# Two-layer decoder trunk on one core: a bank of its own for the second half's scale in the heads, own tiles for output-projection and head weights, background steps elsewhere, tables stored by GpSimd

## The chip, the core and the metric

The kernel runs on one core of one Trainium2 chip. The metric is device time in microseconds (us) of one launch. The core's engines are called by the names that the profile uses: PE (TensorE, matrix products), DVE (VectorE), ACT (ScalarE), POOL (GpSimd) and SP (SyncE, which here only starts transfers). Each engine works through its own list of instructions in order; the lists meet in semaphores.

## The reference

Input `x` is one sequence of 512 positions with 1024 channels, `c` one conditioning vector. Everything is float32.

```python
mod = silu(c) @ w_mod[i] + b_mod[i]              # shift, scale and gate, six vectors of 1024 per layer
h = rms_norm(x, norm_mix[i]) * (1 + sc1) + sh1
layer 0: y = stick_breaking_attention(h, w_qkv, w_o)     # 16 heads of 64, causal
layer 1: u = h @ w_in ; y = diagonal complex state space (64 groups of 16 channels, 64 states) + d_skip * u
         z = gelu(y) ; y = (z * sigmoid(z @ w_glu + b_glu)) @ w_o
x = x + g1 * y
h = rms_norm(x, norm_ffn[i]) * (1 + sc2) + sh2
up = causal_conv3(h @ w_up) + conv_b             # 2 x 2816 columns
x = x + g2 * ((silu(gate half) * value half) @ w_down)
out = rms_norm(x, norm_out) * (1 + sc) + sh      # after both layers
```

## The kernel before, in words

Activations lie transposed: `x[k]`, k = 0 to 7, is a tile of 128 channels by 512 positions, and a product's weights are the stationary operand. To keep float32 accuracy every operand is split into a high and a low part, and `mm3` (L160, L163, L164) makes one product out of three matmuls: high by high, high weights by the low part of the activations (`hL`, `gL`), low weights (`*_l`) by the high part. So a weight block of 512 KB takes four steps before PE can use all of it: SP loads it (`*_r`, L152), ACT copies it to the high part (`*_h`, L154), DVE subtracts to the low part (`*_l`, L155). Split weights live in rings of NW = 5 blocks, loaded ones in a ring of 3.

The modulation vectors are matrix-vector products that nobody needs at once. They run in the background: a step `bg` is one load of 512 KB (`wg`, L184) on SP's queue and one DVE instruction (L185) that multiplies and sums it. Where a `bg` call stands in the program decides where that DVE instruction lies in DVE's list.

The stages in order are: norm and q/k/v products with attention windows (to about 250 us); the attention's output projection `w_o`, by `out_proj`; layer 0's conv-FFN, in three groups of 8, 8 and 6 units (a unit is two up blocks, the convolution on ACT and DVE, and the pair `gH`, `gL`; after a group come its down products); the state-space (SSM) layer; layer 1's conv-FFN; the last norm.

**Heads.** The product that follows a norm cannot start before the whole residual stream is known, so it starts in halves of 256 positions. `out_proj` finishes the first half of all tiles, `rstd_stat` sums the squares (`acc`) with a column matmul on PE, takes the root on ACT and finishes on DVE, `rstd_bc` (L275) spreads the result over all partitions with a matmul into a bank `rbc`, and `norm_tile` makes one tile of the normed input: a DVE product with `rbc` (`nt`, L293), two ACT instructions (`hH` L300, and L302), a DVE subtraction (`hL`, L306). `head_mm` makes these tiles in turn and feeds them to the first four up blocks (ffn0, ffn1) or the first blocks of `w_in`. The first HEADK tiles run in halves, the others at full width. Before the change both halves of the scale share one bank.

**Order.** A scheduler with a simulated timeline arranges the instructions of each engine. The program binds it in places: `pe_pin` keeps program order on PE, `follow` keeps it on another engine or queue, `behind_head` and `issue_after` put work behind a named instruction. Constants HEADB, HEADW, UPRE and USTG say behind which product of a head something is put: the second half's scale, the weight splits of the next blocks, the first SSM stages.

**Tables.** During ffn0, POOL computes the SSM tables in two passes into a scratch tile `tb`; each pass stores two blocks of 512 KB to device memory (`sR`, L969), through SP's queue. After the second pass `ball` (L983), which goes into the scratch's space, is loaded and POOL builds `bl` from it, which SP stores to `sB` (L1002).

## Time and profile before

| | us |
|---|---|
| median of 3 runs (lowest, highest) | 1208.41 (1207.86, 1210.76) |
| profiled execution, its own time | 1208.56 |
| its span, first to last instruction | 1206.5 |
| PE busy | 1169.9 (97%) |
| DVE busy | 884.0 (73%) |
| ACT busy | 564.4 (47%) |
| POOL busy | 264.8 (22%) |
| mean granted clock of PE | 0.992 |

Times of the sums in the prediction are those of the profiled execution: 1206.5 us of span and 2.1 us around it. In a row of the timeline stand the start in us, the duration, the engine, the line, the operation, the tiles written and read, the operands' shape and how many instructions the row folds together; brackets give the idle time of that engine just before, and what ended it. In a row of the windows view stand a stretch of time, its length, and for PE, PEld, DVE, ACT and POOL the busy time and the instructions, then the granted clock, the share of the DMA engines and GB/s.

### The profile page before, as it was taken

Reading aid. Unit: us, or ns where it says so; the run is one execution under the profiler, and the core shown is the slowest. Engines: PE = TensorE matmul, PEld = TensorE weight load, DVE = VectorE, ACT = ScalarE, POOL = GpSimd, SP = SyncE. Lnnn points to the kernel's source line nnn. Section 1 sums busy time; section 2 is a strip of 40 time slices with the busy share of each in tenths; the row PEclk is TensorE's granted clock in tenths of the full one; section 3 lists DMA queues with packets and bytes.
Section 4 is the critical chain, followed back from the end, with each engine's and each line's share of the span. In section 5 each row is a group of like instructions: output and inputs, shape, how many; then the busy total and the mean of one; then the engine's idle time right before and its main releaser. Section 6 shows DMA issues by size and latency. Waiting matters only on the chain.

```text
span 1206.5 us, 16354 instructions
## 1 busy us (share of the span) xinstructions
PE 1169.9 (97%) x6182; PEld 960.6 (80%) x6182; DVE 884.0 (73%) x1298; ACT 564.4 (47%) x884; POOL 264.8 (22%) x241
## 2 busy tenths in 40 slices
PE   8999999979999999989999999999999999999997
PEld 6886777668788877868888878789888888888887
DVE  6968988485896489996877579876598457744655
ACT  6756667346553123422445657644554234422443
POOL 1000000000098799999720000000000000000003
PEclk9999999999999999999999999999999999999999
DMA  8875653261244767878754599652157438432222
GB/s 312 311 247 172 194 176 121 62 234 37 70 124 131 251 237 218 249 232 277 251 174 159 171 303 340 212 169 63 66 178 243 123 110 202 157 117 76 79 79 70
DMA packets 93536, 210.99 MB, mean 175 GB/s; under 512 B 19601, under 2 KB 39953, under 8 KB 93458
## 3 DMA queue, kind: packets, MB, share of 16 engines
q1 hardware_dynamic: 85138, 207.86, 54.0%
q10 hardware_dynamic: 8320, 2.10, 0.8%
q8 instruction: 48, 0.79, 0.3%
q14 instruction: 30, 0.25, 0.1%
HBM read 188.68 MB, written 21.24 MB: 174 GB/s over the span
## 4 chain that ended last, share of the span: by engine, by line
PE 66%; DVE 12%; DMA 7%; POOL 6%; issue 3%; ACT 3%; SPq 1%; POOLq 0%; ACTq 0%; DVEq 0%
PE up L163 10%; PE up L164 10%; PE up L160 10%; PE dn L160 5%; PE dn L163 5%; PE dn L164 5%; DMA wg<-in_w_modT_dram 3%; DVE wg L185 2%; DVE up_l L155 2%; PE wos L160 1%; DVE ca L445 1%; PE wos L164 1%; PE wos L163 1%; DVE om L728 1%; PE o L758 1%
## 5 line engine op out<-in xcount | busy, mean ns | idle before, releaser
L164 PE MATMUL up<-hH,up_l 128*128 128x512 f32 (+1 forms) x692 | 264.4, 384 | 4.3 <-DVE up_l L155 4.2
L163 PE MATMUL up<-hL,up_h 128*128 128x512 f32 (+1 forms) x692 | 264.3, 384 | 0.4 <-DVE hL L306 0.2
L160 PE MATMUL up<-hH,up_h 128*128 128x512 f32 (+1 forms) x692 | 260.7, 384 | 1.2 <-ACT hH L300 1.1
L445 DVE SCALAR_TENSOR_TENSOR ca<-up,small,ca 128x511 f32<-128x511 f32 (+1 forms) x176 | 131.4, 747 | 81.8 <-ACT ca L443 78.9
L185 DVE SCALAR_TENSOR_TENSOR wg<-wg,cact 128x1024 f32<-128x1024 f32 x96 | 123.8, 1305 | 43.9 <-DMA wg<-in_w_modT_dram 43.7
L164 PEld LDWEIGHTS up<-hH,up_l 128*128 128x128 f32 x692 | 130.0, 188 | 32.0 <-DVE up_l L155 6.4
L163 PEld LDWEIGHTS up<-hL,up_h 128*128 128x128 f32 x692 | 130.0, 188 | 26.0 <-DVE hL L306 0.9
L160 PEld LDWEIGHTS up<-hH,up_h 128*128 128x128 f32 x692 | 127.9, 188 | 28.1 <-ACT hH L300 1.5
L163 PE MATMUL dn<-gL,dn_h 128*128 128x512 f32 (+1 forms) x394 | 145.0, 368 | 2.7 <-DVE gL L460 2.7
L160 PE MATMUL dn<-gH,dn_h 128*128 128x512 f32 (+1 forms) x394 | 145.2, 370 | 0.5 <-ACT gH L459 0.5
L164 PE MATMUL dn<-gH,dn_l 128*128 128x512 f32 (+1 forms) x394 | 144.8, 368 | 0.0
L154 ACT ACTIVATE up_h<-up_r 128x1024 fp32r<-128x1024 f32 x84 | 88.3, 1053 | 118.1 <-PE dn L163 39.3
L155 DVE TENSOR_TENSOR up_l<-up_r,up_h 128x1024 fp32r<-128x1024 f32 x84 | 127.9, 1523 | 21.3 <-ACT up_h L154 15.2
L1342 POOL TENSOR_SCALAR xa<-x,Anorm_out 128x256 f32<-128x256 f32 x7 | 5.7, 819 | 577.7 <-ACT dn_h L154 562.8
L443 ACT ACTIVATE ca<-up,small 128x512 f32<-128x512 f32 x88 | 67.9, 771 | 95.0 <-PE up L164 95.0
L163 PEld LDWEIGHTS dn<-gL,dn_h 128*128 128x128 f32 x394 | 74.4, 189 | 15.1 <-DVE gL L460 3.0
L160 PEld LDWEIGHTS dn<-gH,dn_h 128*128 128x128 f32 x394 | 74.5, 189 | 13.6 <-ACT gH L459 0.9
L164 PEld LDWEIGHTS dn<-gH,dn_l 128*128 128x128 f32 x394 | 74.6, 189 | 12.2
L336 DVE SCALAR_TENSOR_TENSOR x<-dn,mod,x 128x512 f32<-128x512 f32 (+1 forms) x55 | 37.3, 678 | 60.8 <-PE dn L164 60.8
L452 ACT ACTIVATE ca<-ca 128x512 f32<-128x512 f32 x44 | 27.9, 633 | 89.7 <-DVE ca L445 88.0
L154 ACT ACTIVATE dn_h<-dn_r 128x1024 fp32r<-128x1024 f32 (+1 forms) x48 | 46.6, 982 | 49.1 <-PE dn L163 35.4
L155 DVE TENSOR_TENSOR dn_l<-dn_r,dn_h 128x1024 fp32r<-128x1024 f32 (+1 forms) x48 | 63.9, 1331 | 2.7 <-ACT dn_h L154 2.5
(306 smaller groups left out, 2256.1 us busy)
## 6 DMA issues: line engine op xcount, KB each, us to landing
wg<-in_w_modT_dram SPq DMA_DIRECT2D x96, 512.0 KB
up_r<-in_w_up_dram SPq DMA_DIRECT2D x84, 512.0 KB
dn_r<-in_w_down_dram SPq DMA_DIRECT2D x32, 512.0 KB
wgs<-in_w_modT_dram SPq DMA_DIRECT2D x16, 512.0 KB
dn_r<-in_w_down_dram SPq DMA_DIRECT2D x16, 384.0 KB
wv_r<-in_w_v_dram SPq DMA_DIRECT2D x8, 512.0 KB
wk_r<-in_w_qk_dram SPq DMA_DIRECT2D x8, 512.0 KB
wq_r<-in_w_qk_dram SPq DMA_DIRECT2D x8, 512.0 KB
```

What stands on the lines that cost most here:

```text
L154: order("S", lambda: S.activation(wh[:, :n], raw[:, :n], AF.Copy))
L155: pin["split"] = order("V", lambda: V.tensor_tensor(wl[:, :n], raw[:, :n], wh[:, :n].bitcast(F32), ALU.subtract))
L160: ins = PE.matmul(ps, ah, bh, start=start, stop=False)
L163: PE.matmul(ps, ah, bl, start=False, stop=False)
L164: PE.matmul(ps, al, bh, start=False, stop=stop)
L185: mul = lambda: V.scalar_tensor_tensor(w, w, 1.0, cact, ALU.mult, ALU.mult, accum_out=raw[:, col:col + 1])
L336: add = lambda: V.scalar_tensor_tensor(xs, pv, gate, xs, ALU.mult, ALU.add)
L443: follow("S", lambda: S.activation(ca, ps, AF.Identity, bias=small[:, cb:cb + 1], scale=tapw[2]))
L445: follow("V", lambda: V.scalar_tensor_tensor(ca[:, q:], ps[:, :T - q], tapw[2 - q], ca[:, q:], ALU.mult, ALU.add))
L452: follow("S", lambda: S.activation(cg, cg, AF.Silu))
L728: pin["scan"] = V.tensor_tensor_scan(om[:, :n][:, ::-1], om[:, :n][:, ::-1], maskb[:, T - n:][:, ::-1], 1.0, ALU.mult, ALU.max)
L758: ins = PE.matmul(po[pr][h2 * HD:(h2 + 1) * HD, j * P:], vn[:, j, hd:hd + HD], src, start=j == 0, stop=j == 3)
```

## The change

It has five parts.

1. **Heads.** The second half's scale gets a bank of its own, from the pool of product banks. HEADK goes from 5 to 6 tiles in halves. The normed tiles of the first half are made two ahead of the products that use them. The second half's statistics stand behind the second product of tile 1, before they stood ahead of tile 2. The last two tiles, at full width, are scaled in two halves because the scale lies in two banks. HEADW, UPRE (10 to 12) and USTG (7, 8 to 6, 7) follow.
2. **Weights around w_o.** The last attention window prefetches three blocks of `w_o` and not four, and has 4 background steps and not 6. `out_proj` for `w_o` has tiles of its own for blocks 5 and 6 (over space that attention has left) and loads the first four up blocks itself, as `upo0` to `upo3`, as the other two heads did already. The five background steps inside it are gone.
3. **Background steps.** The seven steps removed there, and one from the second group and one from the third, go elsewhere. ffn0 has 6, 0 and 3 of them in its groups; it had 0, 3 and 4. Others go into the SSM layer's last stages and the tiles behind them.
4. **Tables.** `sR` is stored through GpSimd's own queue, no longer through SP's.
5. **SSM.** `run(2)` in place of `run(1)` puts two units of the GLU product between a scan and the transposes behind it. The loads of the maps (`pB`, `pR`, `pT`, `pC`) are tied into one order.

On DVE, in the `w_o` projection, from the projection's first residual sums to the statistics (`x_78` to `x_85` are the tiles of the residual stream, `wg` the background steps, `acc` the sum of squares), before:

```order
L336 SCALAR_TENSOR_TENSOR x_78<-wo_1985,mod,x_78 128x512
L185 SCALAR_TENSOR_TENSOR wg_2261,modraw<-wg_2261,cact 128x1024
L336 SCALAR_TENSOR_TENSOR x_79<-wo_1991,mod,x_79 128x512
L155 TENSOR_TENSOR wo_l<-wo_r,wo_h 128x1024
L336 SCALAR_TENSOR_TENSOR x_80<-wo_1995,mod,x_80 128x512
L155 TENSOR_TENSOR wo_l<-wo_r,wo_h 128x1024
...
L185 SCALAR_TENSOR_TENSOR wg_2292,modraw<-wg_2292,cact 128x1024
L336 SCALAR_TENSOR_TENSOR x_83<-wo_2339,mod,x_83 128x256
L155 TENSOR_TENSOR up_1_0_l<-up_1_0_r,up_1_0_h 128x1024
L232 TENSOR_TENSOR acc<-acc,sq 128x512
L185 SCALAR_TENSOR_TENSOR wg_2330,modraw<-wg_2330,cact 128x1024
```

and now:

```order
L155 TENSOR_TENSOR wo_l<-wo_r,wo_h 128x1024 x2
L342 SCALAR_TENSOR_TENSOR x_78<-wo_1985,mod,x_78 128x512
L342 SCALAR_TENSOR_TENSOR x_79<-wo_1991,mod,x_79 128x512
L155 TENSOR_TENSOR wo_l<-wo_r,wo_h 128x1024
...
L155 TENSOR_TENSOR upo_l<-upo_r,upo_h 128x1024
L232 TENSOR_TENSOR acc<-acc,sq 128x512
L342 SCALAR_TENSOR_TENSOR x_85<-wo_2336,mod,x_85 128x256
L232 TENSOR_TENSOR acc<-acc,sq 128x512
L342 SCALAR_TENSOR_TENSOR x_83<-wo_2322,mod,x_83 128x256
L232 TENSOR_TENSOR acc<-acc,sq 128x256 x4
```

Two of the three splits of `w_o` stand ahead of the first residual sum, the five background steps are gone, and four splits of up blocks stand ahead of the statistics where there were three.

On DVE, in ffn0's head, around the second half's scale (`dg` is made from it, `nt` and `hL` are the normed tiles), before:

```order
L262 SCALAR_TENSOR_TENSOR ny<-ntm,ny 128x2
L270 TENSOR_SCALAR dg<-consts,ny 128x128 x2
L293 TENSOR_TENSOR nt_2680<-x_82,rbc 128x256
L293 TENSOR_TENSOR nt_2698<-x_78,rbc 128x256
L306 TENSOR_TENSOR hL_2557<-nt_2681,hH_2549 128x256
```

and now:

```order
L295 TENSOR_TENSOR nt_2641<-x_82,rbc 128x256
L308 TENSOR_TENSOR hL_2566<-nt_2610,hH_2558 128x256
L295 TENSOR_TENSOR nt_2659<-x_83,rbc 128x256
L258 TENSOR_SCALAR nv<-stat 128x2
...
L270 TENSOR_SCALAR dg<-consts,ny 128x128 x2
L155 TENSOR_TENSOR up_2_0_l<-up_2_0_r,up_2_0_h 128x1024
L308 TENSOR_TENSOR hL_2568<-nt_2660,hH_2560 128x256
L295 TENSOR_TENSOR nt_2703<-x_78,rbc 128x256
```

The first half's last products with the scale (tiles `x_82` and `x_83`) stand ahead of the second half's statistics; they stood behind them.

On SP, at the end of ffn0's first group (`sR` are the table stores, `up_8` to `up_11` the second group's blocks, `ball` what POOL waits for), before:

```order
L152 DMA dn_0_7_r<-in_w_down_dram 128x1024
L969 DMA sR<-tb 128x4x256 x2
L184 DMA wg_3677<-in_w_modT_dram 128x1024
L152 DMA up_8_0_r<-in_w_up_dram 128x1024
L983 DMA ball<-in_b_re_dram 128x512
L983 DMA ball<-in_b_im_dram 128x512
```

and now:

```order
L152 DMA dn_0_7_r<-in_w_down_dram 128x1024
L184 DMA wg_3704<-in_w_modT_dram 128x1024
L152 DMA up_8_0_r<-in_w_up_dram 128x1024
L184 DMA wg_3739<-in_w_modT_dram 128x1024
L152 DMA up_8_1_r<-in_w_up_dram 128x1024
L184 DMA wg_3780<-in_w_modT_dram 128x1024
L152 DMA up_9_0_r<-in_w_up_dram 128x1024
L985 DMA ball<-in_b_re_dram 128x512
L985 DMA ball<-in_b_im_dram 128x512
```

The stores are gone from SP's queue, and three loads of up blocks and three background loads stand ahead of `ball`.

The diff, cut to its core:

```diff
-HEADK = 5
+HEADK = 6
+HEADS = (1, 2)
 HEADB = (3, 2)
-HEADW = (4, 7, 10, 12)
-UPRE = 10
+HEADW = (4, 8, 11, 13)
+UPRE = 12
-USTG = (7, 8)
+USTG = (6, 7)
...
     def rstd_bc(R, cr, pl, pinned=False):
-        bc = R["bc"].get(0) or bank(pl, "rbc")
+        bc = bank(pl, "rbc")
...
-        pin["nt"] = V.tensor_tensor(t, x[k][:, cr], bc[:, cr], ALU.mult)
+        for part in HALF if cr == FULL and isinstance(bc, dict) else (cr,):
+            src = bc[part.start] if isinstance(bc, dict) else bc
+            pin["nt"] = V.tensor_tensor(t[:, part.start - cr.start:part.stop - cr.start], x[k][:, part], src[:, part], ALU.mult)
...
     def head_mm(R, h, a, b, hd):
         pin["head"] = []
-        for cr in HALF + (FULL,):
-            for k in range(HEADK) if cr != FULL else range(HEADK, KD):
-                if cr.start == 0 and k == 2:
+        todo = [(k, HALF[0]) for k in range(HEADK)] + [(k, HALF[1]) for k in range(HEADK)] + [(k, FULL) for k in range(HEADK, KD)]
+        made = 0
+        for n, (k, cr) in enumerate(todo):
+
+            while made < (min(n + 3, HEADK) if cr == HALF[0] else n + 1):
+                norm_tile(h, todo[made][0], R["bc"], a, b, todo[made][1])
+                made += 1
+            for q, (w, ps) in enumerate(hd):
+                if cr == HALF[0] and (k, q) == HEADS:
                     rstd_stat(R, HALF[1], True)
-                norm_tile(h, k, R["bc"][0], a, b, cr)
-                for q, (w, ps) in enumerate(hd):
-                    if cr == HALF[0] and (k, q) == HEADB:
-                        rstd_bc(R, HALF[1], None, True)
-                    mm3(ps[:, cr], wk(w, k), (h[0][k][:, cr], h[1][k][:, cr]), k == 0 and cr.start == 0, k == KD - 1)
+                if cr == HALF[0] and (k, q) == HEADB:
+                    rstd_bc(R, HALF[1], mm, True)
+                mm3(ps[:, cr], wk(w, k), (h[0][k][:, cr], h[1][k][:, cr]), k == 0 and cr.start == 0, k == KD - 1)
...
-        getw = getw or (lambda mt: load_w(wsrc(mt), n=n, name=f"{nm}{mt}"))
+        getw = getw or (lambda mt: load_w(wsrc(mt), n=n, name=f"{nm}{mt}", own=own if mt in (whole, whole + 1) else None))
...
                     gs.append(unit_out(i, i - i0, av, split_next))
-                    if l or i - i0 < (0, 3, 4)[gi]:
+                    if l or i - i0 < (8, 0, 3)[gi]:
                         bg(BGU if l else 1, lined=True)
...
-            part.append([load_w(wsrc(3), name="wo3"), None])
             with behind_head([pin["scan"]]):
-                bg(6, False)
-            window(8, wo_units(range(KPRE), (3,)) + wo_units(range(KPRE, 7), range(4)))
-            acc2 = new_acc()
-            R = out_proj(wsrc, list(zip(oh, ol)), mcol(0, 2, 0), acc2, "wo", part=[(w, ps, 7) for w, ps in part], after=lambda: bg(BGW))
+                bg(4, False)
+            window(8, wo_units(range(KPRE, 7), range(3)))
+        acc2 = new_acc()
+        with ExitStack() as oc:
+            own = oc.enter_context(tc.tile_pool(name="wox", bufs=1, reuse_waits="tile"))
+            own.tile([P, 4, D], F32, tag="past", name="past")
+            R = out_proj(wsrc, list(zip(oh, ol)), mcol(0, 2, 0), acc2, "wo", part=[(w, ps, 7) for w, ps in part], own=own,
+                         head=([up_src(0, q, s) for q in range(2) for s in range(2)], "upo"))
...
-                    SP.dma_start(sR[hb * 4:(hb + 1) * 4, :, ri, :].rearrange("b p n -> p b n"), tb[:, ri].rearrange("p (b q) c -> p b (q c)", b=4))
+                    G.dma_start(sR[hb * 4:(hb + 1) * 4, :, ri, :].rearrange("b p n -> p b n"), tb[:, ri].rearrange("p (b q) c -> p b (q c)", b=4))
...
                     if s_ < 8:
                         st_scan(s_)
-                        load_out(s_)
                     if s_ + 1 < 8:
                         load_scan(s_ + 1)
+                    if s_ < 8:
+                        load_out(s_)
...
-                    run(1)
+                    run(2)
                     st_tr(s_ - 2)
                     if s_ >= 8:
                         with behind_head([pin["comb"]]):
-                            bg(12 - s_, False)
+                            bg(4, False)
...
                 gz.append((gh, gl))
+                if mt >= len(gb):
+                    bg(2)
```

More of the change, by code (lines that the diff above doesn't have):

```diff
@@ L58 @@
 NU = 4
-NPRE = 4
+NPRE = 3
 KPRE = 5
@@ L66 @@
 BGA = 5
-BGW = 1
 ZM = ((1, 0), (1, 1), (3, 0), (3, 1))
@@ L339, in resid, with out_proj @@
             acc_sq(acc2, mt, cr)
-    def out_proj(wsrc, rhs, gcol, acc2, nm, tail=TAIL, perm=False, n=D, after=lambda: None, part=(), last=None, head=None, getw=None, step=lambda: None):
+    def out_proj(wsrc, rhs, gcol, acc2, nm, tail=TAIL, perm=False, n=D, after=lambda: None, part=(), last=None, head=None, getw=None, step=lambda: None, own=None):
         nk = len(rhs)
@@ L480, in ffn @@
                 if gi == 0:
-                    if l:
-                        hx, ws = pin["hw"]
-                        hd = [(q, s, ws[2 * q + s], bank(name=f"up{l}_{q}_{s}")) for q in range(2) for s in range(2)]
-                    else:
-                        hx = None
-                        hd = [(q, s) + up_w(q, s) for q in range(2) for s in range(2)]
+                    hx, ws = pin["hw"]
+                    hd = [(q, s, ws[2 * q + s], bank(name=f"up{l}_{q}_{s}")) for q in range(2) for s in range(2)]
                     head_mm(R, h, a, b, [q[2:] for q in hd])
-                    if hx:
-                        hx.close()
+                    hx.close()
                     for q in range(4):
```

10 lines of the change are left out of this document (4 added, 6 removed).

## The prediction, made before the changed kernel ran

> **What bounds the kernel now.** I read the page's busy times first, then the timeline of PE alone for each place where PE stood idle, then the timelines of the engines named as releasers there.
>
> ```profile
> PE 1169.9 (97%) x6182; PEld 960.6 (80%) x6182; DVE 884.0 (73%) x1298; ACT 564.4 (47%) x884; POOL 264.8 (22%) x241
> ```
>
> PE is the bound: it is idle for 1206.5 − 1169.9 = 36.6 us in all. The change takes no matmul away, so what it can win is this idle time, and what the clock loses behind it. The waits of PE on which the sum rests:
>
> ```profile
> 251.52 0.39 PE L164 MATMUL wo<-hH,wo_l 128*128 128x256 f32 x1 [1.05 <-DVE wo_l L155]
> 269.20 1.02 PE L253 MATMUL stat<-ones,acc 128*128 128x1 f32 x4 [6.15 <-DVE acc L232]
> 285.72 0.73 PE L160 MATMUL up<-hH,up_h 128*128 128x256 f32 x4 [1.15 <-ACT hH L300]
> 326.82 0.50 PE L164 MATMUL up<-hH,up_l 128*128 128x512 f32 x1 [0.89 <-DVE up_l L155]
> 444.19 0.50 PE L164 MATMUL up<-hH,up_l 128*128 128x512 f32 x1 [1.59 <-DVE up_l L155]
> 451.71 0.50 PE L164 MATMUL up<-hH,up_l 128*128 128x512 f32 x1 [1.00 <-DVE up_l L155]
> 475.25 0.50 PE L164 MATMUL up<-hH,up_l 128*128 128x512 f32 x1 [0.70 <-DVE up_l L155]
> 518.59 0.49 PE L160 MATMUL dn<-gH,dn_h 128*128 128x512 f32 x1 [0.49 <-ACT gH L459]
> 521.77 0.50 PE L163 MATMUL dn<-gL,dn_h 128*128 128x512 f32 x1 [2.68 <-DVE gL L460]
> 669.65 0.74 PE L160 MATMUL u<-hH,win_h 128*128 128x256 f32 x4 [1.15 <-ACT hH L300]
> 695.67 1.15 PE L1123 MATMUL pv<-u,pB 128*64 128x64 f32 x32 [0.91 <-issue]
> 713.72 0.66 PE L1197 MATMUL pz<-consts,yn 128*128 128x128 f32 x4 [1.45 <-ACT yn L1192]
> 757.93 0.66 PE L1197 MATMUL pz<-consts,yn 128*128 128x128 f32 x4 [1.10 <-ACT yn L1192]
> 840.15 0.74 PE L160 MATMUL up<-hH,uph_h 128*128 128x256 f32 x4 [1.15 <-ACT hH L300]
> ```
>
> The bracket is the idle time and who ended it. These make 21.5 us in five places: the end of `w_o`, the three heads (285, 669, 840), ffn0's groups, and the SSM layer. The rest is the start and the tail, which the change does not touch, and waits below 0.4 us. Two of the waits also cost clock; the windows view shows the granted clock next to last but two:
>
> ```profile
> 270.00:280.00 10.00, 10.00 (x71) 9.95 (x71) 6.10 (x19) 5.15 (x11) 0.00 (x0) 0.83 0.28 84
> 440.00:450.00 10.00, 8.37 (x50) 5.92 (x48) 8.12 (x7) 3.69 (x5) 9.69 (x7) 1.00 0.93 312
> 520.00:530.00 10.00, 8.23 (x42) 6.05 (x43) 10.00 (x11) 2.28 (x3) 7.86 (x6) 0.83 0.97 307
> ```
>
> Behind the waits of 6.15 and 2.68 us stands 0.83, around the wait of 1.59 us 1.00. A clock of 0.83 over 10 us is 1.7 us of matmul time; a little of that lies on the wait itself, so I take 1.5 us each.
>
> The Trainium skill (TensorE: Matmul & The Clock Gate, Part 1) says that the array falls to half rate after an idle window of about 3.4 us whose start is not tied to the program. The trace agrees for the wait of 6.15 us and differs for 2.68, which is shorter and was still followed by 0.83; the measurement decides. By the page alone the second 1.5 us could not be counted on, and the forecast below would be 1.5 us longer.
>
> **The end of w_o.** DVE is the late engine here.
>
> ```profile
> 247.78 0.75 DVE L336 SCALAR_TENSOR_TENSOR x<-wo,mod,x 128x512 f32<-128x512 f32 x1 [2.11 <-PE wo L164]
> 248.45 1.22 DVE L185 SCALAR_TENSOR_TENSOR wg<-wg,cact 128x1024 f32<-128x1024 f32 x1
> 249.59 0.75 DVE L336 SCALAR_TENSOR_TENSOR x<-wo,mod,x 128x512 f32<-128x512 f32 x1
> 266.53 1.22 DVE L185 SCALAR_TENSOR_TENSOR wg<-wg,cact 128x1024 f32<-128x1024 f32 x1
> 267.67 1.85 DVE L232 TENSOR_TENSOR acc<-acc,sq 128x256 f32<-128x256 f32 x4
> ```
>
> From 247.78 to the sums of squares at 267.67 DVE never idles, and five background steps lie in between, each taking 249.59 − 248.45 = 1.14 us of its list: 5.7 us removed. A fourth up split is added ahead of the statistics, 1.14 us (a split is the same 128x1024 pass). Two of the splits of `w_o` now stand ahead of the first residual sum, where DVE idled 2.11 us; one of them, 1.14 us, pays for the added split, and I leave the second out because its weights may land late. So the statistics start 5.7 us earlier, at 263.5. PE has nothing to do from 269.20 − 6.15 = 263.05, and without the wait at 251.52 from 262.0. A wait of 1.5 us is left, nearer to the 1.59 us that left the clock alone than to 2.68. Gain: 5.7 + 1.5 of clock = **7.2 us**. Bounds: the splits don't fit into the idle time and the clock still falls, 5.7 − 2.3 = 3.4; the wait goes altogether, 6.15 + 1.05 + 1.5 = 8.7.
>
> **The heads.** The wait before the second half, in the order rbc on PE, `nt` on DVE, `hH` on ACT, PE; then the spacing of two half-width and of two full-width matmuls:
>
> ```profile
> 283.98 0.59 PE L275 MATMUL rbc<-dg,ones 128*128 128x256 f32 x2
> 284.61 0.75 DVE L293 TENSOR_TENSOR nt<-x,rbc 128x256 f32<-128x256 f32 x2 [1.30 <-PE rbc L275]
> ...
> 287.48 0.28 PE L163 MATMUL up<-hL,up_h 128*128 128x256 f32 x1
> 287.60 0.28 PE L164 MATMUL up<-hH,up_l 128*128 128x256 f32 x1
> ...
> 526.92 0.39 PE L163 MATMUL dn<-gL,dn_h 128*128 128x512 f32 x1
> 527.15 0.40 PE L164 MATMUL dn<-gH,dn_l 128*128 128x512 f32 x1
> ```
>
> DVE waits 1.30 us for the spread scale although the next tile is still one of the first half, which needs the old one: it is behind in DVE's list and reads the same bank. From rbc to PE's next matmul it is 285.72 − 283.98 = 1.74 us. With a bank of its own the first-half tile is ready before, and PE has the 12 matmuls of tile 5 between rbc and the second half: 12 × 0.12 = 1.44 us of cover, 0.3 us left. So 1.15 − 0.3 = 0.85 per head, 2.6 for three. One more tile in halves costs 24 × 0.12 − 12 × 0.23 = 0.12 per head, 0.36 in all. Gain **2.2 us**. Bounds: the wait only moves, −0.4; all of it goes, 3.45 − 0.36 = 3.1.
>
> **Group 0 of ffn0.** The wait at 326.82 came from a split that started late; two splits more stand inside the head now. Gain **0.9 us**, bounds 0 and 0.9. Against it stand six background steps that are new here, five of them ahead of the last `gL` of the group:
>
> ```profile
> 371.08 1.53 DVE L445 SCALAR_TENSOR_TENSOR ca<-up,small,ca 128x511 f32<-128x511 f32 x2 [1.45 <-ACT ca L443]
> 374.39 0.69 DVE L460 TENSOR_TENSOR gL<-gm,gH 128x512 fp32r<-128x512 f32 x1
> 380.93 0.75 DVE L336 SCALAR_TENSOR_TENSOR x<-dn,mod,x 128x512 f32<-128x512 f32 x1 [2.31 <-PE dn L164]
> 381.60 1.32 DVE L185 SCALAR_TENSOR_TENSOR wg<-wg,cact 128x1024 f32<-128x1024 f32 x1
> ```
>
> The last `gL` ends at 375.08. The first down product ends at 380.93 and reads it about three matmuls (0.7 us) earlier, so there are 5.1 us of slack, and DVE idled another 1.45. Five steps at 1.32 us are 6.6 us: the cover just holds, cost 0. If each takes 2.31 us, as one does below beside a busy POOL, it is 11.6 us and PE waits 5.0 us.
>
> **Groups 1 and 2 of ffn0.** SP's queue and DVE, as they fall behind:
>
> ```profile
> 395.54 3.88 SPq L969 DMA_DIRECT2D sR<-tb x2
> ...
> 404.44 1.22 DVE L185 SCALAR_TENSOR_TENSOR wg<-wg,cact 128x1024 f32<-128x1024 f32 x1 [16.28 <-DMA wg<-in_w_modT_dram]
> ...
> 441.85 2.29 DVE L155 TENSOR_TENSOR up_l<-up_r,up_h 128x1024 fp32r<-128x1024 f32 x1 [5.17 <-PE up L164]
> 445.76 2.31 DVE L185 SCALAR_TENSOR_TENSOR wg<-wg,cact 128x1024 f32<-128x1024 f32 x1
> 457.48 1.31 DVE L185 SCALAR_TENSOR_TENSOR wg<-wg,cact 128x1024 f32<-128x1024 f32 x1
> ```
>
> SP stands at the two table stores until POOL has the table; everything behind them, the next `wg` and the blocks of group 1, comes late, and DVE idles 16.28 us that it lacks later. From 441.85 it is behind PE: one unit with a background step takes DVE 457.48 − 445.76 = 11.7 us against 48 × 0.23 = 11.0 of PE. The change lets three background loads and three up blocks go ahead of the point where SP now stops (`ball`, which needs the stores landed), and takes the steps out of group 1: 11.7 − 2.3 = 9.4 us per unit, so DVE gains 1.6 us a unit. The waits at 444, 451 and 475 go, 3.3 us. In group 2 three steps are left, each unit 0.7 us longer than PE's, 2 us in all, which I leave on the 3.2 us at 518 and 521; then the clock holds, 1.5. Gain 3.3 + 1.2 + 1.5 = **6.0 us**. Bounds: nothing changes, 0; all goes, 6.46 + 1.5 = 8.0. A last up block behind `ball` may still be late: I take **1 us** off, from 0 to 3.
>
> **The table stores.** No transfer issued by GpSimd is in this trace, so the price has to be bounded by SP's:
>
> ```profile
> 370.80 0.38 SPq L969 DMA_DIRECT2D sR<-tb  x1
> ...
> 374.44 0.13 POOL L958 MEMSET tb<- 128x16 f32 x1 [3.67 <-DMA sR<-tb]
> ```
>
> Issue to landing is 3.6 us here, and POOL waits for it. POOL is off PE's chain until `sB`, so a few microseconds more cost nothing: price 0, from −1 (a gain, as the first stores leave SP's queue too) to the second rival's.
>
> **The SSM layer.** Two more units of the first product stand ahead of the first scan, 6 × 0.23 = 1.4 us of cover for the 0.91 at 695. One more unit of the GLU product between scan and transposes is 0.7 us of cover for 1.45 and 1.10. At 713 ACT's list now has the transposed tile's copy `yn` ahead of the four copies that delayed it, which I count as the rest of 1.45. Gain 0.91 + 1.45 + 0.69 = **3.0 us**, bounds 1 and 3.5. The five steps put into this layer are 5 × 1.14 = 5.7 us of DVE work, hidden behind PE's products of the last GLU blocks as long as their loads are there; if one is not, the splits behind it wait for some 1 us. The map loads keep nearly their old order on SP. Both 0, from −1 to 1.
>
> **Sum.** 7.2 + 2.2 + 0.9 + 6.0 − 1 + 3.0 = 18.3 us. 1208.56 − 18.3 = 1190.3, I say **1190**. The profiled execution is 0.15 us above the median of 1208.41.
>
> **Rivals.**
>
> *The lag comes back (about 1198).* DVE's work is the same, only its place differs. For it: 2.31 us for a step beside a busy POOL. Then group 0 ends 5.0 us late, and half of group 1 and 2's gain, 3 us, goes too: 1190 + 8 = 1198. Against it: the step at 381.60 took 1.32 us with POOL at work.
>
> *The stalls only move (about 1207).* PE is at 97%, and each place made faster could meet the next late load. For it: DVE is full at 520 to 530. The heads and w_o keep 2 us at most. Against it: the largest wait, 6.15 us, ends in a list from which 5.7 us of unneeded work is removed.
>
> *The stores by GpSimd land late (about 1215).* SP now stops at `ball` until they have landed, and behind it stand `up_9_1` and all of group 1. Unit 9 runs before the row at 444.19; its second block is used from about 438, and needs load, copy and split, 3.6 + 1.1 + 2.3 us, and places in three queues, so I put its last issue at about 422. `ball` went at about 403 before (395.54 + 3.88 + 3.6), so 19 us of delay are covered. From there each microsecond counts, and from 19 + 18 = 37 us it is slower than before; at 44 us 1215. That is four stores at 11 us and more each instead of 3.6. For it: DVE is busy throughout. Against it: nothing in these rows is near such a size. The Trainium skill (SBUF — State Buffer, the trap that it calls "DVE blocks DMA") says that GpSimd cannot write the descriptors of its own transfers while DVE runs certain two-port operations, and advises SP or ACT for plain transfers. No run here shows it yet.
>
> **Chances and range.** Forecast (1184 to 1194) 0.55; below 1184, all upper bounds together, 0.05; lag comes back (1194 to 1203) 0.25; stalls move 0.08; late stores 0.07. Range 1184 to 1203, which leaves 0.2 outside. Faster by over 0.3% means below 1204.8, about what can be told from no change here: 0.85; within 0.3% 0.08; slower 0.07.
>
> **What would show it.** The wait at `stat` below 2 us and no 0.83 behind it; no wait over 0.5 us at the first second-half matmul of each head; no wait of DVE for `wg` near 404, no wait on `up_l` in 440 to 480, and under 2.5 us at the group 2 down products; `pz` waits below 0.5 us. Wrong would be: a new wait on `gL` near 375, POOL waiting much more than 3.7 us for `sR`, or a low clock at 270 to 280 again.

## The result, and the profile after

The changed kernel takes 1195.19 us (median of 4 runs, 1194.98 to 1196.58), against 1209.59 us of the kernel before in the same comparison: a ratio of 0.988, 95% interval 0.9854 to 0.9905, so 14.4 us faster. Forecast were 1190 us and 18.3 us of gain, range 1184 to 1203. Time and sign held, in part by luck: two large terms of the sum were wrong, in opposite directions.

The page's first lines and the waits of PE after the change:

```profile
span 1192.1 us, 16454 instructions
...
PE 1167.3 (98%) x6218; PEld 962.2 (81%) x6218; DVE 883.4 (74%) x1310; ACT 562.9 (47%) x890; POOL 270.4 (23%) x245
```

```profile
264.45 0.60 PE L253 MATMUL stat<-ones,acc 128*128 128x1 f32 x4 [1.97 <-DVE acc L232]
318.45 0.50 PE L164 MATMUL up<-hH,up_l 128*128 128x512 f32 x1 [0.90 <-DVE up_l L155]
372.71 0.50 PE L160 MATMUL dn<-gH,dn_h 128*128 128x512 f32 x1 [0.91 <-ACT gH L462]
373.88 0.50 PE L163 MATMUL dn<-gL,dn_h 128*128 128x512 f32 x1 [0.67 <-DVE gL L463]
447.88 0.50 PE L160 MATMUL up<-hH,up_h 128*128 128x512 f32 x1 [0.98 <-ACT up_h L154]
450.21 0.50 PE L164 MATMUL up<-hH,up_l 128*128 128x512 f32 x1 [1.59 <-DVE up_l L155]
514.57 0.50 PE L163 MATMUL dn<-gL,dn_h 128*128 128x512 f32 x1 [2.50 <-DVE gL L463]
744.67 0.66 PE L1199 MATMUL pz<-consts,yn 128*128 128x128 f32 x4 [0.47 <-ACT yn L1194]
778.07 0.50 PE L163 MATMUL wos<-gzL,wos_h 128*128 128x512 f32 x1 [0.64 <-DVE gzL L1283]
```

Of the waits that the prediction listed, those of the heads are gone, the 6.15 us at the statistics are 1.97, and most of the SSM layer's are gone. But ffn0 still has its waits: 0.90 where there was 0.89, 1.58 new at the first group's down products, 2.57 and 2.50 in the second group where there were 3.29 and 3.17.

Waits alone don't add up to the gain, since a lower clock and many idle times below 0.2 us belong to it. So here is the program cut at the first product of each stage, read from PE's timeline (us; the second profile of the changed kernel is another execution of it):

| stage, from its first product to the next one's | before | changed | changed, second profile |
|---|---|---|---|
| start to the first v product | 18.2 | 18.2 | 20.3 |
| q, k, v, attention, w_o, up to the statistics | 251.0 | 246.2 | 245.2 |
| statistics to the first up product of ffn0 | 8.6 | 6.7 | 6.7 |
| ffn0 group 0, up (with the head) | 92.6 | 90.8 | 90.8 |
| ffn0 group 0, down | 43.6 | 45.8 | 44.9 |
| ffn0 group 1, up | 94.4 | 94.4 | 93.9 |
| ffn0 group 1, down | 50.4 | 49.5 | 52.1 |
| ffn0 group 2, up and down | 97.0 | 96.8 | 96.8 |
| SSM layer, statistics to its output projection | 131.1 | 124.5 | 124.5 |
| SSM output projection | 38.7 | 39.8 | 39.9 |
| statistics, then FFN 1 group 0, up (with the head) | 97.8 | 96.0 | 95.9 |
| the rest, up to the last product's start | 276.5 | 276.5 | 276.5 |

From the first to the second column it is −4.7 −1.9 −1.8 +2.2 −0.9 −0.1 −6.7 +1.1 −1.8, without rounding −14.7 us: the whole gain.

**The end of w_o** on DVE after the change:

```profile
245.31 2.36 DVE L155 TENSOR_TENSOR wo_l<-wo_r,wo_h 128x1024 fp32r<-128x1024 f32 x2 [0.26 <-ACT wo_h L154]
248.75 1.43 DVE L342 SCALAR_TENSOR_TENSOR x<-wo,mod,x 128x512 f32<-128x512 f32 x2 [1.08 <-PE wo L164]
...
262.93 1.85 DVE L232 TENSOR_TENSOR acc<-acc,sq 128x256 f32<-128x256 f32 x4
```

Two splits run ahead of the first residual sum, and the four sums of squares start at 262.93 instead of 267.67.

**ffn0, where nothing was won.** SP's queue, then POOL, then DVE:

```profile
385.72 0.33 SPq L152 DMA_DIRECT2D up_r<-in_w_up_dram  x1
405.95 0.33 SPq L985 DMA_DIRECT2D ball<-in_b_re_dram  x1
...
435.52 6.37 SPq L1004 DMA_DIRECT2D sC<-cl  x4
...
443.15 1.32 SPq L152 DMA_DIRECT2D up_r<-in_w_up_dram  x3
```

```profile
367.51 0.12 POOL L960 MEMSET tb<- 128x16 f32 x1 [3.01 <-DMA sR<-tb]
...
388.84 1.60 POOL L851 TENSOR_TENSOR tb<-tt 128x256 f32<-128x256 f32 x1
...
402.38 0.77 POOL L971 DMA_DIRECT2D sR<-tb  x1 [0.30 <-POOL tb L854]
403.15 0.30 POOL L978 MEMSET kz<- 128x224 f32 x1
```

```profile
414.92 1.79 DVE L185 SCALAR_TENSOR_TENSOR wg<-wg,cact 128x1024 f32<-128x1024 f32 x1 [17.05 <-DMA wg<-in_w_modT_dram]
...
447.86 2.29 DVE L155 TENSOR_TENSOR up_l<-up_r,up_h 128x1024 fp32r<-128x1024 f32 x1 [5.26 <-ACT up_h L154]
```

SP now stands at `ball` from 386 to 406 where it stood at the stores up to 395.5; DVE idles 17.05 us where it idled 16.28. PE reaches group 1 at 407.8 where it reached it at 414.1, but `ball` goes out 3 us later than before (405.95 against 402.79). Behind that, four stores of `sC` stand in a row on SP and keep it for 6.4 us, and the next three up blocks leave at 443; the first of them is the one for which PE waits at 447.88.

### The profile page after: what moved, and what is told of

Its sections match the earlier page's. It is cut to its first block, busy times and chain, and to the rows that moved or that the text cites. A ratio compares the mean times of both kernels' runs of the same rounds, so it can differ in the third digit from the quotient of the medians.

```text
span 1192.1 us, 16454 instructions
## 1 busy us (share of the span) xinstructions
PE 1167.3 (98%) x6218; PEld 962.2 (81%) x6218; DVE 883.4 (74%) x1310; ACT 562.9 (47%) x890; POOL 270.4 (23%) x245
## 4 chain that ended last, share of the span: by engine, by line
PE 72%; DVE 9%; POOL 8%; DMA 5%; issue 2%; ACT 2%; SPq 1%; POOLq 0%; DVEq 0%; ACTq 0%
PE up L160 9%; PE up L163 9%; PE up L164 9%; PE dn L160 5%; PE dn L163 5%; PE dn L164 5%; PE o L756 2%; DVE ca L448 1%; DMA wg<-in_w_modT_dram 1%; PE k L160 1%; PE t L738 1%; PE u L163 1%; PE u L160 1%; PE u L164 1%; PE wo L160 1%
## 5 line engine op out<-in xcount | busy, mean ns | idle before, releaser
L164 PE MATMUL up<-hH,up_l 128*128 128x512 f32 x640 | 250.0, 391 | 2.5 <-DVE up_l L155 2.5
L160 PE MATMUL up<-hH,up_h 128*128 128x512 f32 x640 | 250.3, 392 | 1.0 <-ACT up_h L154 1.0
L163 PE MATMUL up<-hL,up_h 128*128 128x512 f32 x640 | 249.9, 390 | 0.0
L164 PEld LDWEIGHTS up<-hH,up_l 128*128 128x128 f32 x640 | 120.4, 188 | 28.4 <-DVE up_l L155 3.3
L160 PEld LDWEIGHTS up<-hH,up_h 128*128 128x128 f32 x640 | 120.5, 188 | 27.7 <-ACT up_h L154 1.4
L163 PEld LDWEIGHTS up<-hL,up_h 128*128 128x128 f32 x640 | 120.5, 188 | 24.4
L154 ACT ACTIVATE up_h<-up_r 128x1024 fp32r<-128x1024 f32 x80 | 84.2, 1052 | 106.1 <-DMA up_r<-in_w_up_dram 57.6
L155 DVE TENSOR_TENSOR up_l<-up_r,up_h 128x1024 fp32r<-128x1024 f32 x80 | 120.3, 1504 | 11.9 <-ACT up_h L154 11.0
```

Of the source, the lines that this page charges most:

```text
L154: order("S", lambda: S.activation(wh[:, :n], raw[:, :n], AF.Copy))
L155: pin["split"] = order("V", lambda: V.tensor_tensor(wl[:, :n], raw[:, :n], wh[:, :n].bitcast(F32), ALU.subtract))
L160: ins = PE.matmul(ps, ah, bh, start=start, stop=False)
L163: PE.matmul(ps, ah, bl, start=False, stop=False)
L164: PE.matmul(ps, al, bh, start=False, stop=stop)
```

## The experiments

Their theories: the gain comes from the w_o lists, the heads and the SSM covers; ffn0's gain is lost because the place where SP stands only moved. The rivals are with each run. The changed kernel gave 1195.19 us above and 1197.62 in a second comparison, so single undo steps are read from the stage times too.

**heads_old: the old heads in the changed kernel.**

```diff
-HEADK = 6
+HEADK = 5
-HEADW = (4, 8, 11, 13)
+HEADW = (4, 7, 10, 12)
...
-        bc = bank(pl, "rbc")
+        bc = R["bc"].get(0) or bank(pl, "rbc")
...
```

with the loop of `head_mm` and the single product of `norm_tile` as before.

> The changed kernel with the heads as before: one bank for both halves of the scale, five tiles in halves, no tile made ahead. Theory (the shared bank made the first half's last tile wait, 1.15 us in each of three heads): the waits of about 1.15 us at the first matmul of the second half come back in all three heads, 1195.2 + 4 = 1199 us (1198 to 1200). Rival (what the heads win is lost again at the next late weight): 1195 to 1196 us, with the waits back and others gone.

Measured: 1206.36 us, ratio 0.9968 (0.9952 to 0.9983). The waits at the second halves are back:

```profile
282.69 0.74 PE L160 MATMUL up<-hH,upo_h 128*128 128x256 f32 x4 [1.15 <-ACT hH L300]
667.70 0.74 PE L160 MATMUL u<-hH,win_h 128*128 128x256 f32 x4 [1.15 <-ACT hH L300]
837.45 0.74 PE L160 MATMUL up<-hH,uph_h 128*128 128x256 f32 x4 [1.15 <-ACT hH L300]
```

The waits came back as expected; the size did not, 11 us against 4. By stages the two FFN heads cost 1.5 and 1.8 us. The SSM stage after its statistics is 4.6 us longer, but of that a wait for `pB` at 738 (1.48 us) is not the head's. The rest of the 11 us is in places that the heads don't touch: this profile starts 3.0 us later and has the lower clock behind the statistics, 1.5 us.

**heads_only: the new heads in the kernel before.** The same edit the other way.

> The kernel before with the new heads alone (own bank, six tiles in halves, tiles two ahead). Theory (the heads are worth more than the waits of 1.15 us, since the two-ahead tiles also take the small waits of 0.2 to 0.4 us and the gaps below): the first-unit stages of both FFNs 1.7 us shorter each and the SSM stage 2.4 us shorter, 1209.3 - 5.5 = 1204 us (1203 to 1205.5). Rival (2.2 us as predicted): 1207 us.

Measured: 1203.76 us, ratio 0.9951 (0.993 to 0.9971), −6.3 us. Stages: ffn0's first −1.5, FFN 1's first −1.9, the SSM stage −2.8, together −6.2. Total and stages agree: three heads are worth about 6 us, not 2.2.

**wo_bg: the five background steps back in the projection.**

```diff
-    R = out_proj(..., part=[(w, ps, 7) for w, ps in part], own=own,
+    R = out_proj(..., part=[(w, ps, 7) for w, ps in part], own=own, after=lambda: bg(1),
-                    if l or i - i0 < (8, 0, 3)[gi]:
+                    if l or i - i0 < (3, 0, 3)[gi]:
```

> The changed kernel with the five background steps back in the w_o projection, and five fewer in ffn0's first group. Theory (five steps of 1.14 us on DVE's list ahead of the statistics made the wait): PE's wait at the statistics goes from 2.0 to about 7.5 us and the clock falls to 0.83 behind it, +7 us, and the waits at the end of ffn0's first group (1.6 us) go: about 1201 us (1199 to 1203). Rival (the own tiles and the early splits, not the steps, took the wait away): wait below 4 us, 1195 to 1197 us.

```profile
270.25 1.01 PE L253 MATMUL stat<-ones,acc 128*128 128x1 f32 x4 [6.55 <-DVE acc L232]
```

Measured: 1198.11 us, ratio 0.9909 (0.9875 to 0.9944). The four runs are 1201.35, 1194.78, 1202.68 and 1194.86 us, and the profile is of the first, so the total alone tells nothing against the changed kernel; the stages do. The wait is back (6.55 us, expected 7.5), and the waits at group 0's down products are gone (that stage takes 43.6 us as before the change, against 45.8 and 44.9). Against heads_old, which started equally late, the statistics come 3.7 us later. So the steps cost about 4 us where they stood and give 1 to 2 back where they went: smaller than the 7 expected, since five steps in group 0 are not free.

**own_off: no own tiles for blocks 5 and 6 of w_o.**

```diff
-... own=own if mt in (whole, whole + 1) else None
+... own=None
```

> The changed kernel without the own tiles for blocks 5 and 6 of w_o; everything else stays. Theory (two of the splits can only run ahead of the first residual sum because of these tiles): the splits move behind it, a wait of about 1 us at a product of w_o comes back and the wait at the statistics grows from 2.0 to about 4 us with the lower clock behind it, 1198 to 1200 us. Rival (the five steps were all): 1195 to 1197 us.

```profile
266.72 1.01 PE L253 MATMUL stat<-ones,acc 128*128 128x1 f32 x4 [4.33 <-DVE acc L232]
```

Measured: 1199.63 us, ratio 0.9929 (0.9906 to 0.9951). The wait at the statistics grows from 1.97 to 4.33 us, the stage behind it to 9.7 us with a clock of 0.83; the wait at a product of w_o did not come back (below 0.2 us). The tiles and the steps both carry the gain at this place.

**ssm_old: the SSM covers undone.**

```diff
-UPRE = 12
-USTG = (6, 7)
+UPRE = 10
+USTG = (7, 8)
...
-                    run(2)
+                    run(1)
```

> The changed kernel with ten units ahead of the first scan in place of twelve, one unit of the GLU product between scan and transposes in place of two, and the first stages placed as before. Theory (more product units ahead of a wait cover it): the waits of 0.9 us at the first pv and of about 1.1 to 1.4 us at two pz come back, SSM stage 119 to 123 us, 1198 us (1197 to 1199.5). Rival (the order of the map loads or the head made that gain): 1195 to 1196 us.

```profile
691.50 1.15 PE L1125 MATMUL pv<-u,pB 128*64 128x64 f32 x32 [1.25 <-issue]
708.99 0.66 PE L1199 MATMUL pz<-consts,yn 128*128 128x128 f32 x4 [0.86 <-ACT yn L1194]
753.47 0.66 PE L1199 MATMUL pz<-consts,yn 128*128 128x128 f32 x4 [0.71 <-ACT yn L1194]
```

Measured: 1198.59 us, ratio 0.9907 (0.988 to 0.9935). The SSM stage takes 4.2 us more; the output projection takes 0.9 less, and the wait at 778 is gone. Net 3.3 us, as expected.

**map_old: the map loads not tied.** The four `follow("P", ...)` are plain loads again, and `load_out` stands ahead of `load_scan`.

> The changed kernel with the SSM map loads not tied and in the old places. Both theories expect no difference, since the loads stand almost in the same order on SP's queue: 1195 to 1198 us, SSM stage 119 to 121.5 us. A gain or loss over 2 us would show that the order mattered.

Measured: 1197.11 us, ratio 0.9908 (0.9877 to 0.9939); SSM stage, here and below from its first product to its output projection, 119.8 us against 119.2. No difference that can be told.

**sr_on_sp and sr_on_sp2: the table stores back on SP.**

```diff
-                    G.dma_start(sR[hb * 4:(hb + 1) * 4, ...
+                    SP.dma_start(sR[hb * 4:(hb + 1) * 4, ...
```

> The changed kernel with the table stores back on SP's queue. Theory (the stores as such cost the same on either queue; what counts is that up_8_1 and up_9_0 now stand ahead of SP's stop): SP stands at the stores until about 399 us, up_8_1 goes after it, PE waits 2 to 5 us more in group 1, 1197 to 1200 us. Rival (SP's stop lies ahead of ball in both, and nothing changes): 1194.5 to 1196 us. Second rival (the transfers by GpSimd are the slower ones): 1191 to 1194 us.

Measured: 1194.98 us, ratio 0.988 (0.9861 to 0.9899). The total is that of the rival, "nothing changes", but the profile says otherwise. SP's queue and PE:

```profile
392.84 3.88 SPq L971 DMA_DIRECT2D sR<-tb  x2
399.98 0.33 SPq L985 DMA_DIRECT2D ball<-in_b_re_dram  x1
...
433.29 1.20 SPq L1004 DMA_DIRECT2D sC<-cl  x2
...
435.22 0.39 SPq L152 DMA_DIRECT2D up_r<-in_w_up_dram  x1
437.73 1.17 SPq L1004 DMA_DIRECT2D sC<-cl  x2
```

```profile
440.20 0.50 PE L164 MATMUL up<-hH,up_l 128*128 128x512 f32 x1 [0.39 <-DVE up_l L155]
512.40 0.50 PE L163 MATMUL dn<-gL,dn_h 128*128 128x512 f32 x1 [0.25 <-DVE gL L463]
726.97 1.15 PE L1125 MATMUL pv<-u,pB 128*64 128x64 f32 x32 [1.41 <-DMA pB<-sB]
```

An up block now leaves between two pairs of `sC`, the waits at 448 and 450 are gone and 2.50 us became 0.25. Group 1 takes 91.4 + 45.7 = 137.1 us against 143.9 and 146.0, and 144.8 in the kernel before: 7.7 us won on that one, in the place where the prediction looked for 6.0. What the changed kernel does not have of it, 6.8 us or more, is lost here elsewhere: +1.6 at group 0's down products, +2.1 in the SSM stage (the wait for `pB`), +1.5 behind the statistics. The theory that this run would be slower fell by its total, but what it names is there at a smaller size: `up_8_1` goes behind SP's stop, in DVE's list a background step whose load was late stands ahead of its split, and PE waits 0.82 us for it (2.17 in the second profile), where 2 to 5 were expected:

```profile
417.75 0.50 PE L164 MATMUL up<-hH,up_l 128*128 128x512 f32 x1 [0.82 <-DVE up_l L155]
```

Is that an accident of one execution? A second profile:

> The changed kernel with the table stores back on SP's queue, once more, for a second profile. Theory (with the stores on GpSimd's queue POOL and SP's later transfers come so that four sC stores stand in a row ahead of an up block, and that costs what the moved steps win): group 1 of ffn0 with its down products takes about 137 us again, against 144 to 146 with the stores on GpSimd; 1193 to 1195 us, part of it given back at the first group's down products and in the SSM stage. Rival (the first profile was an accident of the execution): 143 us or more in that group.

Measured: 1195.22 us, ratio 0.9875 (0.9849 to 0.9901); group 1 takes 93.6 + 46.3 = 139.9 us, the SSM stage 123.3. It repeats at a smaller size: 139.9 lies between the 137 of the theory and the 143 of its rival, 4 to 6 us below the changed kernel's two profiles.

**late4_bg6 and late4_bg6_pool: a faster version, with the stores on SP and on GpSimd.** On the stores-on-SP kernel:

```diff
-            pin["hw"] = head_w(*head)
+            late = head[0][3:] if head[1] == "upo" else []
+            pin["hw"] = head_w(head[0][:len(head[0]) - len(late)], head[1])
...
-                mid[STATK] = lambda: rstd_stat(R, ca, True)
+                def stat():
+                    ins = rstd_stat(R, ca, True)
+                    for src in late if head else []:
+                        with tc.issue_after(ins.ins):
+                            pin["hw"][1].append(load_w(src, name=f"{head[1]}3"))
+                mid[STATK] = stat
...
-                bg(4, False)
+                bg(6, False)
...
-                    if l or i - i0 < (8, 0, 3)[gi]:
+                    if l or i - i0 < (6, 0, 3)[gi]:
```

> A version that should be faster than both: the changed kernel with the table stores back on SP, the fourth up split behind the statistics in place of ahead of them, and two background steps moved from ffn0's first group into attention's last window, where DVE idled 6.6 us. Theory: the wait at the statistics 2.0 - 1.1 = 0.9 us with the clock held (-1.1, and -1.5 where it had fallen), the waits of 1.6 us at the first down products gone, and in groups 1 and 2 the 5 us that the stores on SP showed in the profile: about 1190 us (1187 to 1193). Rival (what is won in one stage is lost to a later wait): 1194 to 1196 us.

Measured: 1190.08 us, ratio 0.9838 (0.9818 to 0.9858): faster than the kernel before, and 7.5 us faster than the changed kernel in the same comparison (1197.62, ratio 0.99, 0.9874 to 0.9925). The wait at the statistics is below 0.25 us, and the stage behind it takes 6.7 us. The rest went not as expected. Group 0's down products take 47.9 us: ACT waits 4.45 us for a down block, whose load stands on SP's queue behind a table store, and PE behind it 1.56 us for `gH`. Group 1 takes 140.6, and its wait for `gL` is not gone (2.73 us at 510.70).

> The faster version with the table stores on GpSimd's queue again. Theory as for the run before: group 1 of ffn0 with its down products 143 to 146 us against 140.6, the waits for up_h and up_l near 448 back with the lower clock, 1190.1 + 3 = 1193 us (1192 to 1196). Rival (the queue of the stores does not matter): 1189 to 1191 us.

Measured: 1191.58 us, ratio 0.9852 (0.9832 to 0.9872); the intervals of the two overlap. By stages the queue matters again in both directions:

| | group 0 down | group 1 up and down | SSM stage |
|---|---|---|---|
| stores by GpSimd: changed; second profile; late4_bg6_pool | 45.8; 44.9; 43.6 | 143.9; 146.0; 145.9 | 119.2; 119.2; 119.2 |
| stores by SP: sr_on_sp; sr_on_sp2; late4_bg6 | 47.4; 45.9; 47.9 | 137.1; 139.9; 140.6 | 121.3; 123.3; 122.0 |

With the stores on SP group 1 is 3 to 9 us shorter in every pair, and the other two stages together are 3 to 7 us longer. The sum hides it. For group 1 the other experiments agree: with the stores on GpSimd all eight profiles (prep_pool_queue left out) lie between 142.6 and 146.6 us. For the SSM stage they don't: wo_bg, with the stores on GpSimd, takes 122.2 us and waits 1.05 us for `pB`, so that loss is not shown to be the queue's.

**prep_pool_queue: SP's stops taken away.** In the changed kernel `ball` and, for the first two blocks, `lam`, `bt`, `bc`, `sB` and one block of `sC` are transferred by GpSimd as well:

```diff
-                SP.dma_start(ball[:, ri]...
+                G.dma_start(ball[:, ri]...
-                tc.keep_in_program_order(SP.dma_start(out, in_))
+                tc.keep_in_program_order((G if goff[0] else SP).dma_start(out, in_))
...
+                goff[0] = bi < 2
```

> The changed kernel with the transfers of the first two blocks of the SSM preparation (ball, lam, bt, bc, sB, the first sC) issued by GpSimd, so that SP no longer stands still for POOL from 386 to 406, 423 to 430 and 435 to 442 us. Theory (SP's stop only moved from the stores to ball, so the up blocks of group 1 still come late): DVE's wait of 17 us for wg goes, the waits of PE at 448 and 450 (2.6 us and 1.5 us of clock) go, 1195.2 - 4 = 1191 us (1189 to 1193). Rival (DVE beside a busy POOL is the limit in group 1, whatever SP does): the waits stay within 1 us, 1194.5 to 1196 us.

```profile
449.33 0.66 PE L996 MATMUL pk<-cl,bd 128*32 128x128 f32 x8 [7.74 <-POOL cl L1057]
454.39 0.66 PE L996 MATMUL pk<-cl,bd 128*32 128x128 f32 x8 [4.40 <-POOL cl L1060]
```

```profile
410.96 0.56 POOL L985 DMA_DIRECT2D ball<-in_b_re_dram  x1 [3.21 <-DMA sR<-tb]
...
416.33 1.06 POOL L849 TENSOR_TENSOR t<-ball,fr 128x512 f32<-128x512 f32 x1 [4.27 <-DMA ball<-in_b_re_dram]
...
447.88 1.40 POOL L1057 TENSOR_TENSOR cl<-t,t 128x576 f32<-128x576 f32 x1
```

Measured: 1204.52 us, ratio 0.9952 (0.9935 to 0.9969), against 1191 expected: a miss. The first half of the theory shows: DVE's wait for `wg` and the waits of up products at 448 and 450 are gone. But each issue takes POOL 0.56 us, it waits 3.21 us for its own stores before it can load, and starts the first block's `cl` at 447.88. In the changed kernel the same instruction, three lines higher in the code, starts 14.7 us earlier:

```profile
433.21 2.29 POOL L1054 TENSOR_TENSOR cl<-t,t 128x576 f32<-128x576 f32 x1
```

PE's small products `pk`, whose place among PE's matmuls is fixed, wait 12.1 us for it. Group 1's chain is as much POOL's as SP's.

**after_again: the changed kernel once more.**

> The changed kernel itself once more, for a second profile beside the experiments. If the stage times of one kernel repeat: PE's wait at the statistics 2.0 us without a lower clock behind it, 0.83 at 450 to 460 and 510 to 520 us, the SSM stage (from its first product to its output projection) 119 us, 1195 us. If they hang on the execution: the stage behind the statistics takes 8.2 us in place of 6.7 with 0.83 in front of it, or the SSM stage 121 us with a wait of 1.4 us for pB, as in the four experiments so far.

Measured: 1197.62 us (1194.34 to 1201.65), ratio 0.99 (0.9874 to 0.9925). Its stages stand in the table above. SSM stage, heads and statistics repeat to 0.1 us, ffn0's groups to 2.6, and the start not at all: over all profiles the first v product stands between 18.0 and 22.3 us. So a difference of 2 us between two medians says little here, while a stage that repeats says much.

## Why the prediction was right and wrong

By the stages, w_o brought 0.6 us less than forecast, the heads 4.0 more, ffn0 without its head 6.7 less (0.8 lost where 0.9 + 6.0 − 1 were to be won) and the SSM layer 0.3 less: 14.7 in place of 18.3.

**The end of w_o: right, 7.2 forecast, 6.6 measured** (4.7 up to the statistics, 1.9 behind them). The remaining wait is 1.97 us, 1.5 was forecast. The step "nearer to the 1.59 us that left the clock alone" was luck: in eight profiles with this wait the stage behind it took 6.7 us three times and 8.2 five times, and both from one kernel (sr_on_sp2 and sr_on_sp).

The traces show what decides it. In windows of 1 us the granted clock is 1.00 or 0.50 except in the one where it changes; 0.83 over 10 us is a stretch of 3.41 us at 0.50. All such stretches of an execution, some of them two or four steps long, lie on one grid with steps of 3.41 us. Here are the step that holds the end of the wait and the step behind it, in the changed kernel and in sr_on_sp, both with the wait of 1.97 us:

```profile
263.23:266.64 3.41, 2.19 (x18) 2.19 (x19) 2.45 (x11) 1.09 (x3) 0.00 (x0) 1.00 0.13 50
266.64:270.05 3.41, 3.41 (x29) 3.36 (x28) 1.66 (x5) 1.14 (x3) 0.00 (x0) 1.00 0.00 0
```

```profile
262.94:266.36 3.42, 1.90 (x16) 1.91 (x17) 2.46 (x11) 1.09 (x3) 0.00 (x0) 1.00 0.22 81
266.36:269.77 3.41, 3.41 (x19) 3.41 (x18) 0.84 (x3) 0.00 (x0) 0.00 (x0) 0.50 0.00 0
```

PE was busy 64% of the step in the one, 56% in the other. From 40 us on the 14 profiles have 25 steps at full clock in which PE was busy less than 49%, and each is followed by 0.50. Of the 4621 with more than 57% none is; of the nine between, four are. (At the start this does not hold: in the changed kernel a step with 93% busy, from 10.6 us, is followed by 0.50.) The wait of 1.59 us that left the clock at 1.00 before lay in a step with 56%; now 0.98 us of idle time stands just ahead of such a wait, the step has 44%, and 0.50 follows (447.55 to 454.37). So a wait of 1.97 us costs 1.5 us of clock or nothing by how it lies on the grid and by what other idle time shares its step, and its place on the grid differs between executions of one kernel. That the Trainium skill (TensorE: Matmul & The Clock Gate, Part 1) calls the clock's window free-running agrees with this; that the window has to be an idle one does not, since one in which PE was 44% busy was enough.

**The heads: right mechanism, mis-sized; 2.2 forecast, 6.2 measured** (stages of heads_only). The term that was mis-sized is "1.15 − 0.3 = 0.85 per head": nothing of the wait is left, and waits went that it does not count. After the change PE runs through:

```profile
278.76 0.59 PE L275 MATMUL rbc<-dg,ones 128*128 128x256 f32 x2
279.01 0.82 PE L160 MATMUL up<-hH,upo_h 128*128 128x256 f32 x4
```

The cover of 12 matmuls was counted, but not that tiles made two ahead also take away the waits between tiles. Their brackets are small: 0.22 and 0.21 us in the FFN heads, 0.21 and 0.36 in the SSM's, where another of 0.24 stayed. The distance between the starts of two matmuls, 0.12 us in this part, shows more. In the kernel before an FFN head has three gaps, of 1.52, 0.50 and 0.53 us; in heads_only two are left, of 0.31 and at most 0.37. That is 1.8 us a head, of which ffn0 loses 0.45 again at its next late split (a wait of 1.34 where there was 0.89). The SSM head had 1.52, 0.50 and 0.64 and has 0.31: 2.1 us; the waits for `pv` and `pz` behind it are 2.83 us in sum where they were 3.46.

**Group 0: wrong, −0.9 forecast, +2.2 at its down products.** The wait at 318.45 is what it was at 326.82, so "two splits more stand inside the head" did not reach it. The cover for five steps "just holds" was too tight: `gL` is late by 0.67 us and `gH` by 0.91. wo_bg, with one step in the group, shows 43.6 us and no wait; so does late4_bg6_pool with four. late4_bg6, with four and the stores on SP, does wait, for a late down block.

**Groups 1 and 2: wrong, 6.0 less 1 forecast, 0.9 won (or 1.2 lost in the second profile).** Two steps failed. First, the waits at 518 and 521 were put down to "group 2", whose three steps should leave 2 us; they stand at the down products of group 1, and no steps are left there (the change takes all three out of this group and one out of the next). Second, and this is the larger, "**the table stores: price 0**". The transfer itself was priced rightly: 3.6 us on POOL's queue,

```profile
sR<-tb POOLq DMA_DIRECT2D x4, 512.0 KB, 3.6
```

and 0.77 us to issue. But with SP free to go on, DVE keeps working while POOL makes its second table. The windows view from the start of that pass to the next `kz`, before, changed, and sr_on_sp:

```profile
374.00:399.00 25.00, 25.00 (x112) 20.71 (x111) 9.54 (x12) 4.15 (x5) 22.72 (x39) 1.00 0.33 112
```

```profile
367.00:403.00 36.00, 34.42 (x151) 27.95 (x150) 27.50 (x33) 10.69 (x12) 33.40 (x40) 1.00 0.60 196
```

```profile
369.00:396.00 27.00, 25.42 (x104) 20.31 (x104) 14.83 (x18) 7.42 (x9) 24.68 (x38) 0.94 0.50 182
```

The third number after the length is DVE's, the fifth POOL's. With DVE busy 38% of the time the pass takes 25 us, with 55% 27 us, with 76% 36 us. The other profiles fit: with the stores on GpSimd, in nine of them, 31.2 to 35.8 us with DVE busy 62 to 89%; with the stores on SP, in five, 24.5 to 26.9 with 37 to 54% (all cut at the first and last instruction of the pass). The same product `tb<-tt` of 128x256 takes POOL 1.60 us at 388.84 now, and before

```profile
389.18 0.73 POOL L849 TENSOR_TENSOR tb<-tt 128x256 f32<-128x256 f32 x1
```

0.73. Beside the slow one runs a DVE split that had started before it and ends 0.60 us ahead of it:

```profile
388.21 1.63 DVE L155 TENSOR_TENSOR up_l<-up_r,up_h 128x1024 fp32r<-128x1024 f32 x1
```

So `ball` goes out at 405.95 instead of 402.79, although PE is 6 us earlier, and what hangs on POOL behind it goes out hardly earlier than before: `sB` at 430.22 against 431.18, the two pairs of `sC` at 435.52 and 440.72 against 436.16 and 440.47. Measured against PE they are some 6 us late, and so are the up blocks after them. The Trainium skill (SBUF — State Buffer, SBUF: two separate sides) says that the port pair shared by DVE and GpSimd is locked by one of them for a whole instruction. The durations agree with it: a slowed product is longer by up to 1.1 us whatever its size (0.25 and 1.34 us for 128x16). No run here isolates the lock. What the page warns of for transfers issued by GpSimd did not show for these stores: they landed in 3.4 to 4.4 us.

Shown is that the queue of the stores decides 3 to 9 us in group 1. That DVE's work beside POOL is how it does so is read from the traces and was not tried by itself. Why the SSM stage is 2 to 4 us longer in the three runs with the stores on SP, and in wo_bg without them (the wait for `pB` among it), is open.

**The SSM layer: right, 3.0 forecast, 3.3 by ssm_old** (2.7 by the stages before and after, less what heads_only shows). The output projection is 1.1 us longer, with a wait for `gzL`. This is not the price of the background steps put into the layer, which the sum took as 0: ssm_old keeps them, and its output projection takes 38.9 us, where it took 38.7 before.

**The rivals.** The one called "the lag comes back", 1198 us, describes ffn0 correctly: group 0 ends late and DVE lags again; its price was missed because the heads brought 4 us more than forecast. Late stores by GpSimd (1215 us) did not happen.

## What to carry to other kernels

A queue that stops at a transfer stops at the next one that needs the same producer: before a wait is counted as gone, follow the producer's list and ask what its work costs when the engines beside it stop idling. Price a pipeline that is filled two ahead by all the waits between its steps and not by the one that stands out. And where a part of a change gains in one stage and loses in another, only an undo run read stage by stage tells them apart; the total here was the same to 0.2 us.

## What was not expected of the hardware

Many of POOL's products take up to 1.1 us longer, whatever their size, while DVE is busy (0.73 and 1.60 us for the same 128x256, 0.25 and 1.34 for a 128x16), so an idle DVE seems to have been a benefit. The clock falls to 0.50, for 3.41 us at least, after a step of its grid in which PE was busy less than about half; so it can fall after 1.97 us of idle time and not in the next execution of the same program. The start of the program varies by 4 us between executions (first product at 18.0 to 22.3 us), more than most edits here are worth.
